# Two feed-forward column groups from seven products of summed blocks instead of eight

## Chip, cores and metric

The kernel runs on one core of a Trainium2 chip. The metric is device time in microseconds (us), the median of several runs of the same program. A core has TensorE (PE in the profile; PEld is its weight load), VectorE (DVE), ScalarE (ACT), GpSimd (POOL) and SyncE (SP, which here issues nearly all DMAs). PE reads operands from SBUF and writes to eight banks of PSUM; a bank holds 128 x 512 float32 numbers.

## What is computed

A trunk of two layers over 256 tokens of width 1024. Each layer is a half-step SwiGLU feed-forward (FFN), a token mixer, and a second FFN, each followed by a layer norm:

```
def swiglu(x, w_gate, w_up, w_down):
    return (jax.nn.silu(x @ w_gate) * (x @ w_up)) @ w_down

for l in range(2):
    x = layer_norm(ALPHA * x + 0.5 * swiglu(x, ffn1_gate[l], ffn1_up[l], ffn1_down[l]), ...)
    mix = ...      # pooling heads and a gated recurrence, then @ w_out[l]
    x = layer_norm(ALPHA * x + mix, ...)
    x = layer_norm(ALPHA * x + 0.5 * swiglu(x, ffn2_gate[l], ffn2_up[l], ffn2_down[l]), ...)
```

The hidden width of an FFN is 2816. All is float32.

## The kernel before

**Numbers in two halves.** PE multiplies in a rounded 32-bit format (`fp32r`). To keep float32 accuracy each operand is split into a high part (a cast on ACT) and a low part (the remainder, a subtraction on DVE); the helper `halves` (lines 115-117) does both. A product is then three matmuls, high x high, high x low and low x high, issued by `mm3` (lines 109-113) for a 128 x 128 by 128 x 512 block.

**Groups.** An FFN works through eleven groups (`NG`) of 256 hidden columns. A group's gate and up columns lie side by side, so 1024 input rows x 512 columns, which is four tiles of 128 x 1024 float32 (512 KB each, two input blocks of 128 rows per tile). The 256 tokens are two row blocks (`hf` 0 and 1). Two forms make a group's gate and up products:

- `G(g, hf)`: tokens of one row block are the stationary operand, the 512 columns move. The result is token-major, so SiLU x up (`hn`) is turned by two PE transposes (`T`, lines 455-463) before the down product can use it.
- `GT(g)`: weights are stationary and the tokens move, both row blocks and both halves at once: 32 matmuls of 512 columns (weights' high part against the tokens' high and low parts) and 32 of 256 columns (weights' low part). The result is already hidden-major and needs no transpose. `gate_turned` (lines 358-370) evacuates it.

`D(g, hf)` is the group's share of the down product for one row block: 12 matmuls of 512 columns, accumulated in PSUM over all groups (pool `psa`).

**Order.** PE runs in the written order (`manual_schedule`). The later three FFNs (all but the first one of layer 0) run `G` for groups 0, 1 and 10 and `GT` for groups 2 to 9; from group 3 on each `GT(g)` is followed by both halves of `D(g-1)`. `Later` is a small queue that counts steps (one tick for each three 512-column matmuls) and puts transposes between them, so many ticks behind what they need. ACT, DVE and SP are ordered by the compiler's list scheduler from priorities: evacuations ahead (`AHEAD`), weight loads behind (`BEHIND`).

**Loads.** `Weight.load` issues one DMA into a buffer of the `raw` pool (five buffers), then the ACT cast and the DVE subtraction into a pair of buffers of a ring: `w` (eight), `x` (two more, within an FFN) for gate and up, `d` (six) for down weights. A ring buffer comes free when PE has done its last matmul on it; a `raw` buffer when both parts have been made. The loads stand in one list for the whole program.

**Banks.** Pool `psg` has four PSUM banks: one for each `G`, four for each `GT`, one for each transpose step.

Of the kernel before, what the change touches and what calls it, by code (L numbers as in the profile page):

```python
# [17 lines left out]
P = 128  # L18
# [15 lines left out]
PAD = 16  # L34
TINY = 2.0 ** -60
NEG = -1e30
RAW, NW, NX, ND = 5, 8, 2, 6
FFN_BELOW = ("xh", "xl", "sil", "hn", "zero")
MIX_BELOW = ("mth", "mtl", "la", "lb", "pw", "v", "P01", "Pm")
AHEAD, BEHIND = 100, 400  # L40
PINNED, STARTED = 4, 4
HT = 6
MAPPED = 13
WARM = 17

# [31 lines left out]
def trunk(ctx: ExitStack, tc: tile.TileContext, t, out: bass.AP):  # L77
# [28 lines left out]
            for g in self.guards:  # L106
                g.__exit__(None, None, None)

    def mm3(ps, lh, ll, wh, wl, start, stop):
        nc.tensor.matmul(ps, lh, wh, start=start, stop=False)  # L110
        nc.tensor.matmul(ps, lh, wl, start=False, stop=False)  # L111
        nc.tensor.matmul(ps, ll, wh, start=False, stop=stop)  # L112
        later.tick()

    def halves(dst_h, dst_l, src):
# [5 lines left out]
    class Weight:  # L121


        def __init__(self, src, ring, bufs, by_hand=False):
            self.src, self.ring, self.bufs, self.by_hand = src, ring, bufs, by_hand
            self.uses = 2
            self.parts = None
            stream.append(self)

        def load(self):  # L130
            p = wp if self.ring == "w" else scope[0]
            older = rings.setdefault(self.ring, []) if p else None
# [44 lines left out]
    place = [0, 1]  # L177

    class Transposed:
        def __init__(self, hf, nat, slots=(), cuts=(0, 4, 8)):  # L180
            self.h, self.l = xth[:, place[hf]], xtl[:, place[hf]]
            self.nat, self.cuts, self.done = nat, list(cuts), 0
            for n in slots:

                later(n - 1, lambda: later(1, self.part))

        def part(self):
            a, b = self.cuts[0], self.cuts[1]
            pt = psg.tile([P, 4 * P], F32, name="gu").rearrange("p (k t) -> p k t", k=4)
            for k in range(a, b):  # L190
                nc.tensor.transpose(pt[:, k - a, :], self.nat[:, k * P:(k + 1) * P], ident)  # L191
            halves(self.h[:, a:b, :], self.l[:, a:b, :], pt[:, 0:b - a, :])
            self.done = b
            self.cuts.pop(0)

    def project(hf, ps, ws):

# [51 lines left out]

    normed = [None]  # L250

    def layer_norm(hf, accs, scale, gb, slots, last=False):
        z = xp.tile([P, D], F32, name="x")
        st = sp.tile([P, 2, 6], F32, name="st")
        mv = sp.tile([P, 2], F32, name="mv")
        rs = sp.tile([P, 1], F32, name="rs")
        for c in range(2):
            cs = slice(c * 512, c * 512 + 512)
            nc.vector.scalar_tensor_tensor(z[:, cs], accs[c], scale, x[hf][:, cs], ALU.mult, ALU.add)
            nc.vector.bn_stats(st[:, c, :], z[:, cs])  # L260
        nc.vector.bn_aggr(mv, st.rearrange("p a b -> p (a b)"))
        nc.vector.tensor_scalar_add(rs, mv[:, 1:2], LN_EPS / ALPHA ** 2)
        nc.gpsimd.tensor_tensor(rs, rs, neghalf[:, 0:1], ALU.pow)
        for c in range(2):
            cs = slice(c * 512, c * 512 + 512)
            nc.vector.scalar_tensor_tensor(z[:, cs], z[:, cs], mv[:, 0:1], gb[0][:, cs], ALU.subtract, ALU.mult)
            normed[0] = nc.vector.scalar_tensor_tensor(z[:, cs], z[:, cs], rs, gb[1][:, cs], ALU.mult, ALU.add)
            if last:
                nc.sync.dma_start(out[hf * P:(hf + 1) * P, cs], z[:, cs])
        x[hf] = z  # L270
        pinned[0] = PINNED
        if not last:
            xT[hf] = Transposed(hf, z, slots)

    def last_norm(hf, scale, gb, parts, half, right):

# [25 lines left out]
    class FFN:  # L302
        def __init__(self, l, w, ln_i, first=False, last=False):
            gu, dn = t["gu"][l, w], t["dn"][l, w]
            self.first, self.last, self.mixer_next = first, last, not w
            self.slots = ((16, 16), (14, 14) if w else (13, 13))
            self.accs = [None, None]
            self.gw, self.dw, self.ht = {}, {}, {}
            self.ln = (l, ln_i)
            self.gb = None  # L310
            for g in range(NG):
                self.gw[g] = []
                for kq in range(4):
                    extra = (4 * g + kq) % (NW + NX) >= NW
                    self.gw[g].append(Weight(gu[g, kq], *(("x", NX) if extra else ("w", NW)), first and g == 0))
                for n in {0: [], 1: [0, 1], 2: [], NG - 1: [NG - 2, NG - 1]}.get(g, [g - 1]):
                    self.dw[n] = [Weight(dn[2 * n + i], "d", ND) for i in range(2)]

        def G(self, g, hf):
            ps = psg.tile([P, 2 * GW], F32, name="gu")  # L320
# [3 lines left out]
        def GT(self, g):  # L324

            later.wait(lambda: self.turned(g - 1) or all((g - 1, hf) in self.ht for hf in range(2)))
            ps = [[psg.tile([P, 2 * S], F32, name="gu") for _ in range(2)] for _ in range(2)]
            n = 0  # L330
            for lo in range(2):
                w = S if lo else 2 * S

                blocks = [[0], [1]] if lo or g == 2 and not self.first else [[0, 1]]
                for block in blocks:
                    for kt in range(KT):
                        later.wait(lambda: min(xT[0].done, xT[1].done) > kt)
# [14 lines left out]
                    if lo:  # L352
                        self.gate_turned(g, block[0], ps[block[0]])

        def turned(self, g):
            return (0 if self.first else 2) <= g < NG - 1

        def gate_turned(self, g, i, ps):
            gate = scope[0].tile([P, S], F32, name="sil", bufs=2)
# [12 lines left out]
        def gate(self, g, hf, ps):  # L372
# [82 lines left out]
        def T(self, g, hf, hn):  # L455
# [5 lines left out]
            with tc.high_priority(offset=AHEAD):  # L461
                halves(hth, htl, pt)
            self.ht[g, hf] = (hth, htl)

        def D(self, g, hf, cols=(0, 1)):
            if self.turned(g):
# [15 lines left out]
            for c in cols:  # L482
                cs = slice(c * 512, c * 512 + 512)
                for i in range(2):
                    mm3(self.accs[hf][c], ht[i][0], ht[i][1], dw[i][0][:, cs], dw[i][1][:, cs],
                        g == 0 and i == 0, i == 1 and g == NG - 1 - (self.last and hf == 1 and c == 1))
            if 1 not in cols:
                return
            for w in self.dw[g]:
                w.used()  # L490
            if g == NG - 1:
                layer_norm(hf, self.accs[hf], 0.5 / ALPHA, self.gb, self.slots[hf], self.last)

        def run(self):
            G, GT, D = self.G, self.GT, self.D
            if self.first:
                self.start()
                D(0, 0)
                D(0, 1)
                GT(2)  # L500
                D(1, 0)
                D(1, 1)
            else:
                G(0, 0)
                G(1, 0)
                D(0, 0)
                G(0, 1)
                G(1, 1)
                D(1, 0)
                D(0, 1)  # L510
                GT(2)
                D(1, 1)
            for g in range(3, NG - 1):
                GT(g)
                D(g - 1, 0)
                if g < NG - 2:
                    D(g - 1, 1)
            G(NG - 1, 0)
            D(NG - 2, 0)
            D(NG - 1, 0)  # L520
            G(NG - 1, 1)
            if self.mixer_next:
                tc.keep_in_program_order(nc.scalar.preload_act_table_set("natural_log_exp_and_others"))
            if self.first:
                with tc.high_priority(offset=-BEHIND):
                    lower_bounds()
            if self.last:

                for g, cols in ((NG - 3, (0,)), (NG - 2, (0,)), (NG - 3, (1,)), (NG - 1, (0,)), (NG - 2, (1,)), (NG - 1, None)):
                    D(g, 1, cols)  # L530
            else:
                for g in range(NG - 3, NG):
                    D(g, 1)

        def end(self, ht, dw):

# [58 lines left out]
    def mixer(l, win, wout):  # L595
# [295 lines left out]
        for hf in range(2):  # L891
# [12 lines left out]
                wout[kt].used()  # L904
            if hf == 0:
                place.reverse()
            layer_norm(hf, accs, 1.0 / ALPHA, gb, (14, 14) if hf else (13, 13))

    phases = []
    for l in range(DEPTH):  # L910
# [88 lines left out]
```

## Time and profile before

| | |
|---|---|
| median of 3 runs | 949.76 us (949.13 to 950.33) |
| the profiled execution | 949.23 us |
| its span, first to last instruction | 947.5 us |
| PE busy | 937.8 us, 4911 matmuls |
| DVE busy | 653.4 us |
| ACT busy | 515.1 us |
| DMA | 180.05 MB, mean 190 GB/s |
| granted PE clock | 0.998 |

The profile follows one execution. A matmul's duration there is the time from its start to the end of its last result; successive matmuls overlap, so what a matmul costs is read from the distance between starts.

### The profile page before, as it was taken

The page shows a single profiled execution, that of the slowest core. Times are in us where ns is not written, and L with a number is a line of the kernel's source. Part 1 is how long each engine was busy: PE and PEld are TensorE (multiplying, and loading weights), DVE is VectorE, ACT ScalarE, POOL GpSimd, SP SyncE. Part 2 cuts the span into 40 slices and gives each one's busy share as a digit, 9 for nine tenths or more (in the row PEclk, how much of TensorE's full clock was granted, in tenths as well). Part 3 has the DMA queues.
Part 4 walks back from the last instruction along what each step waited for, and adds up shares of the span by engine and source line. Part 5 has one row for each costly group of instructions (what it writes and reads, how often), then busy time and mean ns, then how long its engine had stood idle before and what let it go on. Part 6 is the DMA issues. An engine that isn't in the chain of part 4 may idle for free.

```text
span 947.5 us, 13287 instructions
## 1 busy us (share of the span) xinstructions
PE 937.8 (99%) x4911; PEld 803.9 (85%) x4911; DVE 653.4 (69%) x1089; ACT 515.1 (54%) x816; POOL 22.7 (2%) x38
## 2 busy tenths in 40 slices
PE   9999999999999999999999999999999999999996
PEld 7888888888988888888888888888898888888885
DVE  7885666779879765655776565647899797565625
ACT  7765554368546755454546645533975466646420
POOL 0000000000010000000000000000000000000000
PEclk9999999999999999999999999999999999999999
DMA  8987676333627876655446666542417377666301
GB/s 307 319 273 262 239 238 196 105 108 115 228 88 254 300 242 208 211 183 178 139 150 244 221 226 211 166 153 101 150 51 264 118 267 263 221 229 213 114 1 45
DMA packets 50944, 180.05 MB, mean 190 GB/s; under 512 B 6208, under 2 KB 6464, under 8 KB 50880
## 3 DMA queue, kind: packets, MB, share of 16 engines
q1 hardware_dynamic: 50544, 178.55, 55.9%
q8 instruction: 38, 0.62, 0.3%
q0 software_dynamic: 192, 0.53, 0.2%
q14 instruction: 26, 0.21, 0.1%
q10 hardware_dynamic: 144, 0.13, 0.0%
HBM read 178.14 MB, written 1.05 MB: 189 GB/s over the span
## 4 chain that ended last, share of the span: by engine, by line
PE 97%; DVE 1%; DMA 1%; ACT 0%; issue 0%; DVEq 0%; ACTq 0%
PE gu L343 39%; PE acc L112 10%; PE acc L111 10%; PE acc L110 10%; PE gu L110 7%; PE gu L111 7%; PE gu L112 7%; PE gu L837 1%; PE acc L418 1%; PE gu L191 1%; PE acc L763 1%; PE acc L709 1%; DMA raw<-in_wout 1%; PE gu L458 0%; PE gu L442 0%; PE acc L799 0%
## 5 line engine op out<-in xcount | busy, mean ns | idle before, releaser
L116 ACT CAST wh<-raw 128x1024 fp32r<-128x1024 f32 x196 | 205.3, 1053 | 112.0 <-DMA raw<-in_gu 41.7
L117 DVE TENSOR_TENSOR wl<-raw,wh 128x1024 fp32r<-128x1024 f32 x196 | 236.1, 1219 | 21.9 <-ACT wh L116 13.9
L343 PE MATMUL gu<-xt,wh 128*128 128x512 f32 x800 | 187.8, 390 | 0.0
L343 PEld LDWEIGHTS gu<-xt,wh 128*128 128x128 f32 x800 | 150.1, 188 | 31.9
L117 DVE TENSOR_TENSOR dl<-raw,dh 128x1024 fp32r<-128x1024 f32 x88 | 106.7, 1222 | 99.4 <-ACT dh L116 99.4
L116 ACT CAST dh<-raw 128x1024 fp32r<-128x1024 f32 x88 | 92.2, 1052 | 115.3 <-DMA raw<-in_dn 105.5
L110 PE MATMUL acc<-dh,hth 128*128 128x512 f32 x354 | 138.6, 392 | 0.0
L112 PE MATMUL acc<-dh,htl 128*128 128x512 f32 x354 | 137.9, 390 | 0.0
L111 PE MATMUL acc<-dl,hth 128*128 128x512 f32 x354 | 137.6, 389 | 0.0
L110 PE MATMUL gu<-wh,xt 128*128 128x512 f32 x288 | 114.1, 396 | 0.0
L111 PE MATMUL gu<-wl,xt 128*128 128x512 f32 x288 | 112.4, 390 | 0.0
L112 PE MATMUL gu<-wh,xt 128*128 128x512 f32 x288 | 112.4, 390 | 0.0
L343 PE MATMUL gu<-xt,wl 128*128 128x256 f32 x800 | 103.8, 283 | 0.0
L343 PEld LDWEIGHTS gu<-xt,wl 128*128 128x128 f32 x800 | 101.0, 192 | 1.9
L366 DVE TENSOR_TENSOR sil<-gu,sil 128x256 f32<-128x256 f32 x66 | 27.7, 420 | 86.9 <-ACT sil L365 86.7
L112 PEld LDWEIGHTS acc<-dh,htl 128*128 128x128 f32 x354 | 66.5, 188 | 13.8
L110 PEld LDWEIGHTS acc<-dh,hth 128*128 128x128 f32 x354 | 66.6, 188 | 12.1
L111 PEld LDWEIGHTS acc<-dl,hth 128*128 128x128 f32 x354 | 66.5, 188 | 12.2
L112 PEld LDWEIGHTS gu<-wh,xt 128*128 128x128 f32 x288 | 54.1, 188 | 11.7 <-DVE xt L117 0.2
L111 PEld LDWEIGHTS gu<-wl,xt 128*128 128x128 f32 x288 | 54.2, 188 | 10.7
L110 PEld LDWEIGHTS gu<-wh,xt 128*128 128x128 f32 x288 | 54.1, 188 | 10.6
L343 PE MATMUL gu<-xt,xh 128*128 128x512 f32 x256 | 61.3, 390 | 0.0
(187 smaller groups left out, 1071.1 us busy)
## 6 DMA issues: line engine op xcount, KB each, us to landing
raw<-in_gu SPq DMA_DIRECT2D x172, 512.0 KB, 4.4
raw<-in_dn SPq DMA_DIRECT2D x88, 512.0 KB, 4.5
raw<-in_win SPq DMA_DIRECT2D x40, 512.0 KB, 4.1
raw<-in_wout SPq DMA_DIRECT2D x16, 512.0 KB, 5.0
lng<-in_ln_g SPq DMA_DIRECT2D x6, 512.0 KB, 5.4
lnb<-in_ln_b SPq DMA_DIRECT2D x6, 512.0 KB, 6.4
x<-in_first SPq DMA_DIRECT2D x4, 384.0 KB, 3.9
raw<-in_first SPq DMA_DIRECT2D x4, 384.0 KB, 5.5
```

What stands on the lines that cost most here:

```text
L110: nc.tensor.matmul(ps, lh, wh, start=start, stop=False)
L111: nc.tensor.matmul(ps, lh, wl, start=False, stop=False)
L112: nc.tensor.matmul(ps, ll, wh, start=False, stop=stop)
L116: first = nc.scalar.copy(dst_h, src)
L117: return first, nc.vector.tensor_tensor(dst_l, src, dst_h.bitcast(F32), ALU.subtract)
L191: nc.tensor.transpose(pt[:, k - a, :], self.nat[:, k * P:(k + 1) * P], ident)
L343: nc.tensor.matmul(ps[i][part][:, 2 * S - w:], weight.parts[lo][:, c:c + P], x[:, 0:w], start=kt == 0 and not lo, stop=kt == KT - 1 and lo ...
L366: nc.vector.tensor_tensor(dst, p[:, 0:S], dst, ALU.add)
L418: nc.tensor.matmul(ps[i][part][:, 2 * S - w:], ws[k // 2].parts[lo][:, c:c + P], xs[:, 0:w], start=k == 0 and not lo, stop=k == KT - 1 and ...
L709: nc.tensor.matmul(pe[:, a:], lf[hf][c][:, h * P:(h + 1) * P], cumM[:, c, a:], start=True, stop=True)
L763: nc.tensor.matmul(dst[:, 2 * j:2 * j + 2, :], side[:, j, :], E[:, 2 * j:2 * j + 2, t0:t0 + dst.shape[2]], start=True, stop=True)
L837: nc.tensor.matmul(ps[i // 2][:, i % 2, :], w, x, start=kt == 0 and n == 0 and i % 2 == 0, stop=kt == KT - 1 and n == 2 and i % 2 == 1)
```

## The change

In each of the three later FFNs the gate and up products of groups 6 and 7 are made together. Take the 256 tokens as two row blocks, the two groups as two column blocks of 512, and the 1024 input rows as two blocks (the even and the odd blocks of 128). The product of two 2 x 2 block matrices takes eight block products; here it takes seven (the scheme of Strassen and Winograd), some of them of sums and differences of blocks. Of these, three are made in the steps `A6.0` to `A6.3` (9 matmuls each step) and four in `B6.0` to `B6.3` (12 each). Their results are token-major: four `T` steps turn them, at 5, 8, 10 and 11 ticks after the last `B` step.

- The sums of token blocks are made on DVE behind each layer norm that leads into a later FFN (`full_part`), from an ACT copy of the transposed tokens, and are split into `Sh` and `Sl`.
- The sums of weight blocks are made on DVE in the `raw` buffers, ahead of cast and subtraction (`first_sums`, `later_sums`). Steps `A` use six loads and steps `B` eight, where the two groups took eight.
- The order of the later FFNs is written out. The down products of groups 2, 3, 4 and 5 are kept back and stand between and behind the `A` and `B` steps. `D0.0` moves from ahead of `G0.1` to behind `G1.1`.
- Loads are listed in the order in which PE's steps need them, in all four FFNs (`share`). The `x` ring stays in the first FFN alone, with three buffers; the later FFNs have the eight of `w`. `hth` and `htl` have eight buffers each, not six.

The core of the diff:

```diff
-RAW, NW, NX, ND = 5, 8, 2, 6
+RAW, NW, NX, ND = 5, 8, 3, 6
+ORDER = [... for s in (
+    "G0.0 G1.0 G0.1 G1.1 D0.0 D0.1 T2 D1.0 T3 D1.1 T4 D2.0 T5 D2.1 "
+    "A6.0 A6.1 A6.2 A6.3 D3.0 B6.0 D3.1 B6.1 D4.0 B6.2 B6.3 D4.1 D5.0 D5.1 T8 D6.0 D6.1 T9 D7.0 D7.1 D8.0 G10.0 D9.0 D10.0 G10.1 ").split()]
+TURNS = (5,8,10,11)
-HT = 6
+HT = 8
...
+                if self.mix:
+                    self.mix(raw)
                 first, second = halves(wh, wl, raw)
...
             halves(self.h[:, a:b, :], self.l[:, a:b, :], pt[:, 0:b - a, :])
+            if self.full:
+                self.full(a // 4, pt)
...
+    def full_part(n, part, pt):
+        own = scope[0].tile([P, 4, P], F32, name="cb", bufs=4)
+        nc.scalar.copy(own, pt)
+        parts_seen[n, part] = own
...
+        if (1 - n, part) in parts_seen:
+            (a11, a12), (a21, a22) = ([parts_seen[i, part][:, k::2] for k in range(2)] for i in range(2))
+            raw = rawp.tile([P, 4, 2, P], F32, name="raw")
+            for dst, a, b, op in ((0, a21, a22, ALU.add), (2, a11, a21, ALU.subtract), (1, raw[:, 0], a11, ALU.subtract),
+                                  (3, a12, raw[:, 1], ALU.subtract)):
+                nc.vector.tensor_tensor(raw[:, dst], a, b, op)
+            sh, sl = (s[:, :, 2 * part:2 * part + 2] for s in sums[0])
+            halves(sh, sl, raw)
...
+    def first_sums(raw, left):
+        for i in range(2):
+            cs = slice(i * 512, i * 512 + 512)
+            nc.vector.tensor_tensor(raw[:, cs], raw[:, cs], left[i].raw[:, 0:512], ALU.subtract)
+
+    def later_sums(raw, right):
+        if right is None:
+            nc.vector.tensor_tensor(raw[:, 0:512], raw[:, 512:], raw[:, 0:512], ALU.subtract)
+        else:
+            nc.vector.tensor_tensor(raw[:, 0:512], right.raw[:, 0:512], raw[:, 0:512], ALU.add)
+            nc.vector.tensor_tensor(raw[:, 512:], raw[:, 0:512], raw[:, 512:], ALU.subtract)
...
+        def A(self, g, n):
+            if n == 0:
+                later.wait(lambda: not self.pending)
+                self.banks = [psg.tile([P, 512], F32, name="gu") for _ in range(3)]
...
+            mm3(self.banks[0], xth[:, 0, k], xtl[:, 0, k], wh[:, 0:512], wl[:, 0:512], start, stop, True)
+            mm3(self.banks[1], xth[:, 0, k + 1], xtl[:, 0, k + 1], wh[:, 512:], wl[:, 512:], start, stop, True)
...
+            mm3(self.banks[2], *self.sums(0, n), th, tl, start, stop, True)
...
+            with tc.high_priority(offset=AHEAD):
+                c11, self.p5 = (scope[0].tile([P, 512], F32, name="cb", bufs=4) for _ in range(2))
+                nc.scalar.copy(c11, self.banks[0])
+                nc.vector.tensor_tensor(c11, c11, self.banks[1], ALU.add)
+                nc.scalar.copy(self.p5, self.banks[2])
...
+        def B(self, g, n):
+            if n == 0:
+                self.banks[1:2] = [psg.tile([P, 512], F32, name="gu") for _ in range(2)]
+            x, z, w, y = self.banks
...
+            products = [lambda: mm3(z, *self.sums(2, n), *t3, start, stop, True),
+                        lambda: mm3(y, *self.sums(3, n), *b22, False, stop, True),
+                        lambda: mm3(x, *self.sums(1, n), *t2, False, stop, True)]
+            for m in (2, 0, 1) if stop else (0, 1, 2):
+                products[m]()
...
+            mm3(w, xth[:, 1, 2 * n + 1], xtl[:, 1, 2 * n + 1], *t4, start, stop, True)
...
+            with tc.high_priority(offset=AHEAD):
+                u, v = (scope[0].tile([P, 512], F32, name="cb", bufs=4) for _ in range(2))
+                nc.scalar.copy(u, x)
+                nc.vector.tensor_tensor(v, u, z, ALU.add)
+                nc.vector.tensor_tensor(u, u, y, ALU.add)
+                nc.vector.tensor_tensor(self.p5, self.p5, v, ALU.add)
+                nc.vector.tensor_tensor(v, v, w, ALU.subtract)
...
+        def by_block(self, g):
+            return not self.first and g in (2,8)
```

In the step names a number ahead of the point is the group (6 stands for the pair 6 and 7), the one behind it the row block or, for `A` and `B`, the step; `T2` in this list is `GT(2)`. `by_block` makes `GT(2)` and now `GT(8)` finish one half of the group's high-part matmuls before the other, so that only two banks are needed at first.

More of the change, by code (lines that the diff above doesn't have):

```diff
@@ L107, in close, with mm3 @@
                 g.__exit__(None, None, None)
[L109 to L112, printed above, removed]
+    def mm3(ps, lh, ll, wh, wl, start, stop, more=False):
+        for n, (a, b) in enumerate(((lh, wh), (lh, wl), (ll, wh))):
+            nc.tensor.matmul(ps, a, b, start=start and n == 0, stop=stop and n == 2, skip_group_check=more)
         later.tick()
@@ L272, in layer_norm @@
         if not last:
-            xT[hf] = Transposed(hf, z, slots)
+            xT[hf] = Transposed(hf, z, slots, full=full and (lambda part, pt, n=place[hf]: full(n, part, pt)))
     def last_norm(hf, scale, gb, parts, half, right):
@@ L310, in __init__ @@
             self.gb = None
[L311 to L317, printed above, removed]
+            self.plan = list(self.order())
@@ new lines, in __init__, with share, want @@
+            self.pairs = {step[1] for step in self.plan if step[0] == "A"}
+            self.pending = set()
+            self.share(gu, dn)
+        def share(self, gu, dn):
+            cost = {"G": 24, "GT": 48, "D": 12, "A": 9, "B": 12}
+            wanted, when, start = [], 0, {}
+            def want(src, begin, end, kind=None, mix=None):
+                wanted.append([src, begin, end, kind, mix])
+                return len(wanted) - 1
+            ends = {}
+            for what, g, *rest in self.plan:
+                n = cost[what] // (2 if rest[1:] and rest[1] and len(rest[1]) == 1 else 1)
+                ends[what, g] = when + n
+                when += n
+            when, sets = 0, {}
+            for what, g, *rest in self.plan:
+                n = cost[what]
+                if what == "B":
+                    sets[what, g, rest[0]] = [want(gu[g + 1, rest[0]], when, when + n, None, "right"),
+                                              want(gu[g, rest[0]], when, when + n, None, "left")]
+                elif what == "A":
+                    if not rest[0] % 2:
+                        k = rest[0]
+                        sets[what, g, k] = [want(gu[g, k], when, when + n, None, "keep"),
+                                            want(gu[g, k + 1], when, when + 2 * n, None, "keep"),
+                                            want(gu[g + 1, k:k + 2, :, 0:512].rearrange("k p c -> p k c"),
+                                                 when, when + 2 * n, None, "first")]
+                elif (what, g) not in sets:
+                    begin, end = when, ends[what, g]
+                    if what in ("G", "GT"):
+                        sets[what, g] = [want(gu[g, k], begin, end) for k in range(4)]
+                    elif what == "D":
+                        sets[what, g] = [want(dn[2 * g + i], begin, end, "d") for i in range(2)]
+                when += cost[what] // (2 if rest[1:] and rest[1] and len(rest[1]) == 1 else 1)
+            free = {"w": [-12] * NW, "x": [-12] * (NX if self.first else 0), "d": [-8] * ND}
+            size = {"w": NW, "x": NX, "d": ND}
+            made = []
+            for n, (src, begin, end, kind, mix) in enumerate(wanted):
+                ring = "d" if kind == "d" else "w" if n < 4 or not self.first else min("wx", key=lambda r: free[r][0])
+                free[ring] = free[ring][1:] + [end]
+                how = None
+                if mix == "first":
+                    how = lambda raw, left=made[-2:]: first_sums(raw, left)
+                elif mix == "right":
+                    how = lambda raw: later_sums(raw, None)
+                elif mix == "left":
+                    how = lambda raw, right=made[-1]: later_sums(raw, right)
+                made.append(Weight(src, ring, size[ring], self.first and n < 4, how))
+            for (what, *where), of in sets.items():
+                ws = [made[n] for n in of]
+                if what in ("G", "GT"):
+                    self.gw[where[0]] = ws
+                elif what == "D":
+                    self.dw[where[0]] = ws
+                else:
+                    self.gw[(what, *where)] = ws
@@ new lines, in order @@
+        def order(self):
+            if self.first:
+                yield "G", 0, 0
+                yield "GT", 1
+                yield from (("D", 0, 0), ("D", 0, 1), ("GT", 2), ("D", 1, 0), ("D", 1, 1))
+                for g in range(3, NG - 1):
+                    yield "GT", g
+                    yield "D", g - 1, 0
+                    if g < NG - 2:
+                        yield "D", g - 1, 1
+            else:
+                yield from ORDER
+                if self.last:
+                    yield from (("D", g, 1, cols) for g, cols in ((FINAL[0], (0,)), (FINAL[1], (0,)), (FINAL[0], (1,)),
+                                                                  (NG - 1, (0,)), (FINAL[1], (1,)), (NG - 1, None)))
+                else:
+                    yield from (("D", g, 1) for g in (*FINAL, NG - 1))
+                return
+            yield "G", NG - 1, 0
+            yield "D", NG - 2, 0
+            yield "D", NG - 1, 0
+            yield "G", NG - 1, 1
+            yield from (("D", g, 1) for g in range(NG - 3, NG))
@@ L324, in GT @@
         def GT(self, g):
-            later.wait(lambda: self.turned(g - 1) or all((g - 1, hf) in self.ht for hf in range(2)))
+            later.wait(lambda: not self.pending)
             ps = [[psg.tile([P, 2 * S], F32, name="gu") for _ in range(2)] for _ in range(2)]
@@ L332, in GT @@
                 w = S if lo else 2 * S
-                blocks = [[0], [1]] if lo or g == 2 and not self.first else [[0, 1]]
+                blocks = [[0], [1]] if lo or self.by_block(g) else [[0, 1]]
                 for block in blocks:
@@ L491, in D @@
             if g == NG - 1:
-                layer_norm(hf, self.accs[hf], 0.5 / ALPHA, self.gb, self.slots[hf], self.last)
+                layer_norm(hf, self.accs[hf], 0.5 / ALPHA, self.gb, self.slots[hf], self.last,
+                           None if self.mixer_next else full_part)
         def run(self):
[L495 to L533, printed above, removed]
+            for what, *args in self.plan:
+                if what == "G" and self.first and args[0] == 0:
+                    self.start()
+                elif what == "GT" and self.first and args[0] == 1:
+                    pass
+                else:
+                    getattr(self, what)(*args)
+                if args[:2] == [NG - 1, 1] and what == "G":
+                    if self.mixer_next:
+                        tc.keep_in_program_order(nc.scalar.preload_act_table_set("natural_log_exp_and_others"))
+                    if self.first:
+                        with tc.high_priority(offset=-BEHIND):
+                            lower_bounds()
         def end(self, ht, dw):
```

72 lines of the change are left out of this document (61 added, 11 removed).

## The prediction

> **What bounds the kernel now.** I read the page first: busy times, then the chain that ended last.
>
> ```profile
> span 947.5 us, 13287 instructions
> ...
> PE 937.8 (99%) x4911; PEld 803.9 (85%) x4911; DVE 653.4 (69%) x1089; ACT 515.1 (54%) x816; POOL 22.7 (2%) x38
> ...
> PE 97%; DVE 1%; DMA 1%; ACT 0%; issue 0%; DVEq 0%; ACTq 0%
> ```
>
> PE is the whole chain. Whether it ever waits is read from windows (columns: stretch, length, then busy us of PE, PEld, DVE, ACT and POOL, granted clock, DMA share, GB/s):
>
> ```profile
> 60.00:930.00 870.00, 869.15 (x4549) 745.38 (x4548) 597.87 (x1004) 470.73 (x747) 21.00 (x30) 1.00 0.55 184
> 365.60:382.20 16.60, 16.60 (x90) 14.37 (x89) 9.78 (x15) 8.88 (x14) 0.00 (x0) 1.00 0.72 254
> 329.70:332.50 2.80, 2.80 (x15) 2.31 (x14) 2.80 (x7) 1.95 (x6) 0.00 (x0) 1.00 0.82 278
> 281.00:305.00 24.00, 24.00 (x117) 20.00 (x116) 23.37 (x31) 15.32 (x20) 1.00 (x1) 1.00 0.76 241
> 318.60:343.60 25.00, 25.00 (x142) 21.94 (x141) 16.28 (x22) 16.90 (x26) 0.00 (x0) 1.00 0.74 250
> 0.00:60.00 60.00, 58.94 (x317) 50.44 (x318) 47.53 (x68) 43.59 (x69) 0.74 (x7) 1.00 0.90 312
> ```
>
> PE is idle 0.85 us of 870, at full clock. So only PE work taken out can shorten the kernel, and any wait put in lengthens it. One GT with its two D (16.6 us) leaves DVE 6.8 us free, but around a layer norm (281 to 305) DVE is busy 23.37 of 24.
>
> **PE's price list.** The chain in order of time gives a GT; the timeline of PE gives the rest (start, duration of what is merged in the row).
>
> ```profile
> 365.77 11.11 PE gu L343 x64
> ```
> ```profile
> 274.83 0.39 PE L110 MATMUL acc<-wh,xt 128*128 128x512 f32 x1
> ...
> 283.44 0.39 PE L112 MATMUL acc<-wh,xt 128*128 128x512 f32 x1
> ...
> 296.37 1.04 PE L191 MATMUL gu<-ident,x 128*128 128x128 f32 x8
> ...
> 298.64 0.39 PE L110 MATMUL acc<-dh,hth 128*128 128x512 f32 x1
> ...
> 302.53 0.39 PE L112 MATMUL gu<-wh,xt 128*128 128x512 f32 x1
> 302.76 0.38 PE L458 MATMUL gu<-ident,hn 128*128 128x128 f32 x2
> 302.89 0.48 PE L110 MATMUL gu<-wh,xt 128*128 128x512 f32 x1
> 303.21 0.39 PE L111 MATMUL gu<-wl,xt 128*128 128x512 f32 x1
> ```
>
> - A 512-column matmul: from 274.83 to 283.44 are 38 steps between 39 matmuls, 0.2266 us each (its duration, 0.39, overlaps the next).
> - A T step (two transposes): from the last matmul before it (302.53) to the second behind it (303.21) 0.68 us, where two plain steps take 0.45: 0.23 us.
> - One GT: 11.11 us. One D, 12 matmuls: 2.72 us.
>
> **The sum on PE.** Removed per later FFN: GT(6) and GT(7), 22.22 us. Added: 4 x 9 in A and 4 x 12 in B, 84 matmuls, 19.03 us, and four T, 0.92 us. The D, G, layer norm transposes and the other GT are moved, not changed. Gain 22.22 - 19.03 - 0.92 = 2.27 us, times three FFNs 6.8 us. The profiled execution, 949.23 us, becomes 942.4; the median, 949.76, is 0.53 higher than that execution and becomes 943.0 if PE never waits.
>
> [...] The row of the transposes:
>
> ```profile
> L458 PE MATMUL gu<-ident,hn 128*128 128x128 f32 x40 | 7.7, 272 | 0.0
> ```
>
> Their mean duration is 272 ns. [...]
>
> **What must now be hidden: DVE and loads in the A and B stretch.** The rows of a cast and of DVE's operations (busy us, mean ns of one, idle before), then timeline rows, some of them merged pairs:
>
> ```profile
> L116 ACT CAST wh<-raw 128x1024 fp32r<-128x1024 f32 x196 | 205.3, 1053 | 112.0 <-DMA raw<-in_gu 41.7 <-PE gu L112 27.3 <-PE gu L343 13.6
> L117 DVE TENSOR_TENSOR wl<-raw,wh 128x1024 fp32r<-128x1024 f32 x196 | 236.1, 1219 | 21.9 <-ACT wh L116 13.9 <-PE gu L343 7.1
> L117 DVE TENSOR_TENSOR xt<-gu,xt 128x512 fp32r<-128x512 f32 x20 | 12.9, 683 | 3.4 <-ACT xt L116 3.4
> L366 DVE TENSOR_TENSOR hn<-gu,hn 128x256 f32<-128x256 f32 x66 | 27.3, 414 | 0.0
> ```
> ```profile
> 285.59 1.28 DVE L117 TENSOR_TENSOR xt<-gu,xt 128x512 fp32r<-128x512 f32 x2
> ...
> 299.01 1.28 DVE L117 TENSOR_TENSOR xt<-gu,xt 128x512 fp32r<-128x512 f32 x2
> ...
> 375.34 0.42 DVE L366 TENSOR_TENSOR sil<-gu,sil 128x256 f32<-128x256 f32 x1 [3.31 <-ACT sil L365]
> 375.68 0.41 DVE L366 TENSOR_TENSOR hn<-gu,hn 128x256 f32<-128x256 f32 x1
> ...
> 380.28 2.35 DVE L117 TENSOR_TENSOR wl<-raw,wh 128x1024 fp32r<-128x1024 f32 x2
> ```
>
> Back to back, a weight remainder takes 2.35 - 1.22 = 1.13 us, a 512-wide operation 1.28 - 0.68 = 0.60, a 256-wide one 0.34.
>
> The step with least room is B6.3. Four of the six A loads fit in the ring while GT(5) runs on the other four buffers; the rest start as GT(5) frees them. Its last 16 matmuls are of 256 columns, (11.11 - 32 x 0.2266) / 32 = 0.12 us each, and the first buffer is free after four of them, 1.4 us ahead of its end. From its end to B6.3, PE runs D2.1, A (36), D3.0, B6.0 to B6.2 (36), D3.1 and D4.0: 120 matmuls, 27.2 us; with the 1.4, 28.6 us. Due by then on DVE: two A loads, eight B loads and four down weights, 14 x 1.13 = 15.8 us; the block sums, 2 for R23 (the second `first_sums` load) and 4 x 3 for B, 14 x 0.60 = 8.4; what is left of GT(5)'s evacuation and A's own, 4 x 0.34 + 0.60 + 0.34 = 2.3. Together 26.5 us in 28.6: 93% busy, more than any GT stretch of before, less than the 97% at 281 to 305. At worst each operation costs its mean duration: 14 x 1.219 + 14 x 0.683 + 5 x 0.414 + 0.683 = 29.4 us; at 97% that is 30.3, and B6.3 waits 1.7 us. At best the sums run early, in raw buffers that need no free ring buffer, and it waits nothing. I take 0.5 us for each FFN, nearer the best, since back-to-back rows show what a full DVE does: 1.5 us. The cover is DVE's 6.8 free us in each GT before; if it is gone, PE pays one for one.
>
> [...] The rows show starts 0.08 us ahead of the end before.
>
> Behind B: c11, u, p5 and v need five 512-wide operations (one already counted) and four SiLU products, some 4 us on DVE at high priority. The T steps come 5 to 11 ticks (3.4 to 7.5 us) behind, while D4.1, D5.0 and D5.1 run 8.2 us: nothing. Queued weight work can delay each by at most one 1.22.
>
> ACT gains eight casts and some ten copies over an FFN; it was busy 8.88 of 16.6 us, so nothing. Were that cover gone, a cast would cost 1.05 us.
>
> **Loads.** Six more per FFN, 9.4 MB in all, and `D4.0` now sits inside B, so the two layer norm vectors (two more 512 KB on SP's queue) fall near that stretch.
>
> ```profile
> raw<-in_gu SPq DMA_DIRECT2D x172, 512.0 KB, 4.4
> ...
> lnb<-in_ln_b SPq DMA_DIRECT2D x6, 512.0 KB, 6.4
> ```
>
> The first 60 us moved 312 GB/s, a load each 1.68 us. Sixteen loads by B6.3 take 27 us at that rate, of which up to five wait landed in `raw`: hidden. SP's in-order waits for a raw buffer hold back later loads only. POOL's queue is untouched.
>
> **The start of an FFN.** `full_part` adds 8 x 0.34 + 2 x 1.13 = 5 us of DVE there; the next stretch (318 to 343) has 8.7 free. But D0.0 stood between the second row block's transposes and G0.1 as cover. In the rows above they start at 296.37, D0.0 at 298.64, and the first low part is made by DVE at 299.01 + 0.68 = 299.69. G0.1's third matmul needs it at 298.64 + 0.45 = 299.09: a wait of 0.6 us, in the two FFNs behind a mixer. If the sums (4 x 0.34 + 1.13 = 2.5 us) also come ahead of the second low part, made at 300.29 and needed 2.7 us later than the first: 302.8 against 301.8, 1.0 us. Between 0 (DVE puts it first) and 1.0 I take 0.5, twice: 1.0 us.
>
> **Other moves at nothing.** GT now follows GT with one D between three times per FFN, and A follows GT(5) so; before it was once; the row 329.70:332.50 shows PE full over such a gap, with DVE also full. If a remainder cuts in, 1.13 us each. The smaller ring: with eight buffers a GT's loads start when the GT before the last frees its four, a GT and a D (13.8 us) ahead, and need 4.4 us to land, one cast and 4 x 1.13, some 10 us. Only the list order of the first FFN's loads changes; PE was full there with DMA at 90% of its time (0 to 60), so I cost it at nothing too, where a late load would cost up to the 1.68 us between loads.
>
> Sum: -6.8 + 1.5 + 1.0 = -4.3, the profiled execution 944.9, the median 945.5 us.
>
> **Rivals.**
> - *DVE leaves gaps in the A and B stretch, and it gets slower.* The order on DVE is fixed beforehand and each remainder waits for its cast:
>
> ```profile
> DVE dl L117 <- ACT dh L116: 99.4, 57, 6.4
> ```
>
>   99.4 us of DVE idling of this kind exist already, 1.7 us a time. At 80% busy, 26.5 us take 33.1 and B6.3 waits 4.5 us per FFN: 949.8 - 6.8 + 13.5 + 1.0 = 957.5. It turns slower where the three waits exceed 6.8 + 1.9 - 1.0 = 7.7 us, 2.6 each, that is DVE under 85%. For: the GT row has DVE at 59%. Against: there it has less to do. Chance 0.16.
> - *DVE pays full durations*: waits of 1.7: 949.8 - 6.8 + 5.1 + 1.0 = 949.1, no change. Against: the 2.35 row. 0.07.
> - *Raw buffers bound the loads.* A load of B that waits for its partner holds its buffer for at most 6.4 us to land, 1.7 for the partner, 1.2 for sums, 1.05 and 1.13 for cast and remainder, 11.5 us; were all 14 held so, five buffers would take 32.2 us and be 3.6 late, and at the 4.4 us of a plain load (9.5 us held) 26.6, in time. Half of that, 1.8 late: 949.8 - 6.8 + 5.4 + 1.0 = 949.4, no change. For: sums hold two or three buffers together. Against: down weights have no sums. 0.08.
> - *Transposes cost their duration*: 8 x 0.272 = 2.18 us, gain 1.01 per FFN, 949.8 - 3.0 + 2.5 = 949.3, no change. 0.03.
>
> **How the numbers follow.** 0.2% (1.9 us) is about what a measurement can tell from no change. The forecast has 0.66: 943.0 (no waits) to 947.4, its own range. No change: 0.07 + 0.08 + 0.03 = 0.18. Slower 0.16. The range takes in the no-change cases and ends at 951.5, where the slower one begins, which it leaves out; below it starts at 942.5, half a us under the waitless sum.
>
> **What would show it.** In the profile after: 84 matmuls in 19.0 us of starts for A and B; T steps still at 0.23; DVE over 90% from GT(5) to B6.3; PE idle, if any, in front of B6.3 or G0.1. Wrong it is if PE stops elsewhere, in front of a T or a GT, or if waits exceed 2.6 us per FFN.

## The result and the profile after

The changed kernel takes 945.02 us (median of six), the kernel before 949.29 us on the same chip. One of the six executions ran at a lower granted clock (0.849, 1029 us); without it the median is 944.78 us, and the ratio of the others to the kernel before is 0.9948, 95% interval 0.9934 to 0.9961. The forecast was 945.5. The profiled execution takes 944.78 us, its span is 942.8.

The page after (span; busy times; the chain that ended last):

```profile
span 942.8 us, 13184 instructions
...
PE 932.9 (99%) x4803; PEld 794.6 (84%) x4803; DVE 719.2 (76%) x1176; ACT 540.4 (57%) x837; POOL 23.1 (2%) x38
...
PE 88%; DVE 4%; DMA 4%; issue 1%; ACT 1%; SPq 0%; DVEq 0%; ACTq 0%
```

PE has 108 matmuls fewer and is busy 4.9 us less; DVE has 66 us more to do. The chain shows what that used up: before, it ran through PE for 97% of the span, now for 88%, and the rest is weights on their way through DMA, ACT and DVE.

Windows of the kernel after (columns as in the prediction): the long stretch, and the A and B stretch of the second FFN, from the start of D2.1 to just ahead of the first T step:

```profile
60.00:930.00 870.00, 869.57 (x4470) 740.61 (x4469) 663.71 (x1092) 496.89 (x770) 21.46 (x30) 1.00 0.58 196
369.60:402.00 32.40, 32.40 (x144) 26.65 (x143) 31.07 (x41) 19.61 (x26) 0.00 (x0) 1.00 0.77 248
```

PE stands for 0.43 us of 870, and in the A and B stretch for none, with DVE busy 31.07 of 32.40 us (96%).

PE's timeline after: the layer norm transposes that open and close the second FFN, the ends of the A and B stretch, and the two places where PE waited in a later FFN:

```profile
297.62 1.04 PE L200 MATMUL gu<-ident,x 128*128 128x128 f32 x8
...
369.62 0.39 PE L117 MATMUL acc<-dh,hth 128*128 128x512 f32 x1
...
402.99 0.39 PE L117 MATMUL acc<-dh,htl 128*128 128x512 f32 x1
403.22 0.38 PE L658 MATMUL gu<-ident,cb 128*128 128x128 f32 x2
403.36 0.48 PE L117 MATMUL acc<-dh,hth 128*128 128x512 f32 x1
403.67 0.39 PE L117 MATMUL acc<-dl,hth 128*128 128x512 f32 x1
...
467.18 1.04 PE L200 MATMUL gu<-ident,x 128*128 128x128 f32 x8
...
592.14 0.40 PE L540 MATMUL gu<-xt,wh 128*128 128x512 f32 x1
592.78 1.43 PE L540 MATMUL gu<-xt,wh 128*128 128x512 f32 x5 [0.24 <-DVE htl L122]
...
764.42 0.39 PE L117 MATMUL gu<-wl,xt 128*128 128x512 f32 x1
764.74 0.74 PE L117 MATMUL gu<-wh,xt 128*128 128x512 f32 x2
```

- From 369.62 to 403.22 lie 147 steps (D2.1, A and B with D3.0, D3.1 and D4.0 between them, D4.1 and the first three matmuls of D5.0): 33.60 us, 0.2286 each, against 0.2266 for plain ones. Nothing stands there.
- A T step: 402.99 to 403.67 is 0.68, two plain steps are 0.45: 0.23 us, as before.
- From transposes to transposes the second FFN takes 467.18 - 297.62 = 169.56 us. Before, its rows start at 296.37 (shown in the prediction) and 468.11: 171.74. It is 2.18 us shorter.

```profile
468.11 1.03 PE L191 MATMUL gu<-ident,x 128*128 128x128 f32 x8
```

- The second bank of GT(8) comes 0.64 us after the first matmul (592.14 to 592.78) instead of 0.23: it waits for `htl` of the last T step, whose bank it takes.

From such rows the difference of the two executions, 5.1 us up to the last matmul, splits into:

| | us |
|---|---|
| first FFN (slower first matmuls, 1.89 us for four in place of 1.35; one wait in a GT) | +1.29 |
| first mixer | -0.04 |
| second FFN | -2.18 |
| third FFN (0.52 at GT(8), 0.18 in A) | -1.31 |
| second mixer, which had stood 1.1 us before | -1.07 |
| fourth FFN (0.2 at G0.1) | -1.81 |

Behind the last matmul the changed kernel takes 0.48 us longer to its end (8.49 us, before 8.01), so of the 5.1 us the span keeps 4.7. The rows up to the issue of the output's DMA are alike; the 0.48 us lie between that issue and the end, and why is not settled.

### The profile page after: what moved, and what is told of

Read it like the earlier page. It is cut to its first block, busy times and chain, and to the rows that moved or that the text cites. A ratio compares the mean times of both kernels' runs of the same rounds, so it can differ in the third digit from the quotient of the medians.

```text
span 942.8 us, 13184 instructions
## 1 busy us (share of the span) xinstructions
PE 932.9 (99%) x4803; PEld 794.6 (84%) x4803; DVE 719.2 (76%) x1176; ACT 540.4 (57%) x837; POOL 23.1 (2%) x38
## 4 chain that ended last, share of the span: by engine, by line
PE 88%; DVE 4%; DMA 4%; issue 1%; ACT 1%; SPq 0%; DVEq 0%; ACTq 0%
PE gu L540 28%; PE acc L117 26%; PE gu L117 25%; PE gu L1013 2%; DMA raw<-in_dn 2%; DMA raw<-in_cumM 1%; PE acc L618 1%; DVE wl L122 1%; PE acc L939 1%; DMA raw<-in_gu 1%; PE gu L200 1%; PE acc L885 1%; DVE dl L122 1%; PE gu L658 1%; PE acc L975 0%
## 5 line engine op out<-in xcount | busy, mean ns | idle before, releaser
L121 ACT CAST wh<-raw 128x1024 fp32r<-128x1024 f32 x237 | 248.1, 1053 | 155.6 <-DMA raw<-in_gu 53.2
L122 DVE TENSOR_TENSOR wl<-raw,wh 128x1024 fp32r<-128x1024 f32 x237 | 286.0, 1221 | 36.9 <-ACT wh L121 18.9
L117 PE MATMUL gu<-wh,xt 128*128 128x512 f32 x648 | 213.3, 394 | 0.0
L117 PEld LDWEIGHTS gu<-wh,xt 128*128 128x128 f32 x648 | 121.6, 188 | 25.4 <-DVE xt L122 0.5
L117 PE MATMUL gu<-wl,xt 128*128 128x512 f32 x324 | 126.5, 391 | 0.0
L117 PEld LDWEIGHTS gu<-wl,xt 128*128 128x128 f32 x324 | 61.0, 188 | 12.1
L566 DVE TENSOR_TENSOR sil<-gu,sil 128x256 f32<-128x256 f32 x54 | 22.7, 420 | 61.6 <-ACT sil L565 61.6
L121 ACT CAST hth<-hn 128x256 fp32r<-128x256 f32 x56 | 22.7, 406 | 18.6 <-DVE hn L568 17.9
L576 ACT ACTIVATE sil<-gu 128x256 f32<-128x256 f32 x20 | 7.7, 383 | 43.8 <-PE gu L117 43.6
L565 ACT COPY sil<-gu 128x256 f32<-128x256 f32 x54 | 19.9, 369 | 16.8 <-PE gu L540 16.7
```

The lines of the kernel that those rows point to most:

```text
L117: nc.tensor.matmul(ps, a, b, start=start and n == 0, stop=stop and n == 2, skip_group_check=more)
L121: first = nc.scalar.copy(dst_h, src)
L122: return first, nc.vector.tensor_tensor(dst_l, src, dst_h.bitcast(F32), ALU.subtract)
L565: nc.scalar.copy(dst, p[:, S:2 * S])
L566: nc.vector.tensor_tensor(dst, p[:, 0:S], dst, ALU.add)
```

## Experiments

Ratios are to the kernel before, on the same chip, with a 95% interval. Changes are against the changed kernel.

**The same kernel again**, twice: its ratio beside the other runs.

> The changed kernel itself, once more, as the base for the other runs and as a second look at where its time goes. If the 6.8 us of PE work are the gain and the rest of the ledger (a slower start, one wait of 0.5 us in the first FFN, one of 0.5 us at GT(8) of the second later FFN) belongs to this execution and not to the kernel, those waits come elsewhere or not at all, and the later FFNs again lose 1.8 to 2.2 us each. If the waits belong to the change, they stand in the same places: 0.5 us at 116.7 and at 592.1 us.

> The changed kernel once more, unchanged, as the measure for the two runs beside it on the same chip. Every theory: a ratio to the kernel before of 0.995, about 944 to 945 us.

944.06 us, 0.9951 (0.9939 to 0.9964), and 944.04 us, 0.9939 (0.9927 to 0.9951). A wait at GT(8) came back in both (0.43 and 0.26 us in the third FFN); the one in the first FFN did not, and that FFN was 0.72 and 0.63 us longer than before, not 1.29. The second FFN was 1.57 and 2.12 us shorter, the first with 0.57 us of waits in its GT steps. The 0.48 us behind the last matmul are there in both.

**Groups 6 and 7 as GT again**, without sums of tokens or weights; the rest is kept: written order, load list, ring, buffers.

```diff
-    "A6.0 A6.1 A6.2 A6.3 D3.0 B6.0 D3.1 B6.1 D4.0 B6.2 B6.3 D4.1 D5.0 D5.1 T8 ..."
+    "T6 D3.0 D3.1 T7 D4.0 D4.1 D5.0 D5.1 T8 ..."
```

> Keeps the new order, load list, rings and eight hidden-part buffers, but makes groups 6 and 7 by two GT again, each followed by its down products, and no block sums. Theory (the gain is the matmuls that the seven products spare): PE's work is that of before, so 949.3 us within 1 us. Rival (the new order and load list are worth something themselves): faster than before by over 1 us, about 947, or slower by the lost cover at G0.1, about 950.5.

950.13 us, 1.0014 (1.0001 to 1.0028). The new order and list gain nothing (by the interval they cost 0.1 to 2.7 us). The seven products are the whole gain: 950.13 - 944.06 = 6.1 us.

**Down products not kept back**: D(g-1) behind GT(g) as before, none between A and B, only D5 behind B.

```diff
-    "... T2 D1.0 T3 D1.1 T4 D2.0 T5 D2.1 A6.0 ... A6.3 D3.0 B6.0 D3.1 B6.1 D4.0 B6.2 B6.3 D4.1 D5.0 D5.1 T8 ..."
+    "... T2 D1.0 D1.1 T3 D2.0 D2.1 T4 D3.0 D3.1 T5 D4.0 D4.1 A6.0 ... A6.3 B6.0 B6.1 B6.2 B6.3 D5.0 D5.1 T8 ..."
```

> Keeps the seven products but does not keep the down products back: D follows its GT as before, A and B stand side by side, D5.0 and D5.1 alone come behind. Theory (DVE's work due by B6.3 is hidden only since D2.1, D3 and D4 stand in between): from the end of GT(5) PE passes D4, A and B6.0 to B6.2 in 21.8 us and, with the 1.4 us before it, has 23.2; DVE owes 2 + 8 loads and D5's two, 12 x 1.13 + 14 x 0.60 + 2.3 = 24.3 us, 25.0 at 97%: a wait of some 1.8 us in or ahead of B, and the last two T come before GT(8) with no down product over them, some 0.7 us: 2.5 us per FFN, 7.5 in all, about 952.5. Rival (the order hides nothing that matters): 945 as the changed kernel.

958.01 us, 1.0097 (1.0083 to 1.0112): slower than before, and 5.5 us over what was expected. Its timeline behind B in the second FFN, and windows there:

```profile
406.75 0.39 PE L117 MATMUL acc<-dh,htl 128*128 128x512 f32 x1
407.66 0.77 PE L658 MATMUL gu<-ident,cb 128*128 128x128 f32 x4 [0.52 <-DVE cb L510]
410.53 0.69 PE L658 MATMUL gu<-ident,cb 128*128 128x128 f32 x2 [2.10 <-DVE cb L510]
410.87 1.63 PE L540 MATMUL gu<-xt,wh 128*128 128x512 f32 x3
```
```profile
399.10:406.90 7.80, 7.80 (x37) 6.28 (x35) 6.59 (x8) 4.89 (x6) 0.00 (x0) 1.00 0.92 345
406.90:411.00 4.10, 1.48 (x9) 0.88 (x7) 4.05 (x9) 3.98 (x9) 0.00 (x0) 0.91 0.77 253
411.00:414.50 3.50, 3.50 (x12) 2.79 (x11) 3.50 (x5) 1.93 (x4) 0.00 (x0) 0.61 0.76 206
```

PE does not stop in front of B (no step of A or B is over 0.3 us late) but in front of the T steps, for `cb`: DVE is full (4.05 of 4.10 us) and eight ticks of down products are too few for the products of c11, u, p5 and v. Then comes a cost that no term had: the granted clock falls (0.61 is the mean of the last window), and matmuls start 0.43 us apart instead of 0.23 for some 3 us.

**No down products between A and B, but D4 and D5 behind B**: D3 comes ahead of A.

```diff
-    "... T2 D1.0 T3 D1.1 T4 D2.0 T5 D2.1 A6.0 ... A6.3 D3.0 B6.0 D3.1 B6.1 D4.0 B6.2 B6.3 D4.1 D5.0 D5.1 T8 ..."
+    "... T2 D1.0 D1.1 T3 D2.0 T4 D2.1 T5 D3.0 D3.1 A6.0 ... A6.3 B6.0 B6.1 B6.2 B6.3 D4.0 D4.1 D5.0 D5.1 T8 ..."
```

> As the run with A and B side by side, but D4 comes behind B instead of ahead of A, so that D4.0, D4.1, D5.0 and D5.1 stand behind it (16 ticks for four T steps), and none between A and B. Theory (what the kept-back down products are needed for is the evacuation behind B: copy, four additions and three SiLU products on a full DVE, some 3 us longer than I had it): the waits at T vanish, B waits at most 0.3 us, and the time is the changed kernel's, 944 to 945. Rival (down products between A and B are needed too, for ACT's copies of two banks and for DVE's sums): 1 to 2 us of waits in front of B6.0 or B6.3 per FFN and a slower clock behind them, 948 to 953.

949.57 us, 0.9999 (0.999 to 1.0009): in the range of the rival. The trace is of the longest of twelve executions (947.17 to 951.69 us). Its timeline at B6.3 of the second FFN, and windows ahead of it and behind:

```profile
394.22 0.39 PE L117 MATMUL gu<-wh,xt 128*128 128x512 f32 x1
394.89 0.50 PE L117 MATMUL gu<-wh,Sh 128*128 128x512 f32 x1 [0.28 <-ACT wh L121]
397.12 0.50 PE L117 MATMUL gu<-wl,Sh 128*128 128x512 f32 x1 [1.73 <-DVE wl L122]
```
```profile
371.00:394.50 23.50, 23.50 (x107) 18.77 (x105) 21.76 (x30) 13.86 (x21) 0.00 (x0) 1.00 0.61 200
394.50:403.00 8.50, 6.49 (x21) 4.83 (x21) 7.31 (x9) 5.01 (x6) 0.00 (x0) 0.80 0.94 308
```

This is the wait at B6.3 that the prediction named, 0.44 + 2.01 us, with matmuls 0.43 us apart behind it (1.6 us more; the granted clock is 0.80 in the second window); in the third and fourth FFN PE waits there for 1.5 and 0.8 us. But the run before has no down products between A and B either, and does not wait at B6.3. What differs is how many halves of down products PE has passed by then, and how many are left behind B:

| | ahead of B6.3 | behind B, ahead of GT(8) | where PE waits in the second FFN |
|---|---|---|---|
| not kept back | 10 | 2 | T steps, 0.7 + 2.3 us |
| the changed kernel | 9 | 3 | nowhere |
| D4 and D5 behind B | 8 | 4 | B6.3, 0.44 + 2.01 us |

Ahead of B6.3 the down products stretch the time in which DVE prepares weights; behind B they stretch the time in which it makes the outputs. Both are needed; that those ahead must stand between A and B is not shown.

**Each sum of weight blocks followed by another operation of its size** on the same `raw` part, four such lines:

```diff
             nc.vector.tensor_tensor(raw[:, cs], raw[:, cs], left[i].raw[:, 0:512], ALU.subtract)
+            nc.vector.tensor_tensor(raw[:, cs], raw[:, cs], raw[:, cs], ALU.max)
```

> Behind each block sum of the weights stands one more DVE operation of the same size in place (the maximum of a number with itself): 14 x 0.60 = 8.4 us more DVE work due by B6.3, 16 x 0.60 = 9.6 per FFN. Theory (DVE is 93 to 97% full there, so added work goes one for one into PE's waits once the small room is used): 34.9 us at 97% are 36.0 against 28.6, up to 7.4 us per FFN less what runs early while GT(5) goes on (some 2 us): 5.4 per FFN, 16 in all, about 961. Rival (DVE has room since its sums run far ahead in raw buffers): under 3 us in all, about 947.

970.54 us, 1.0228 (1.0213 to 1.0244), 9.5 us over what was expected. PE's timeline at B6.2 and B6.3, DVE's row at the end of the long wait, and a window behind:

```profile
394.93 0.39 PE L117 MATMUL gu<-wh,Sh 128*128 128x512 f32 x1
396.16 0.50 PE L117 MATMUL gu<-wl,Sh 128*128 128x512 f32 x1 [0.85 <-DVE wl L122]
...
397.20 0.40 PE L117 MATMUL gu<-wh,xt 128*128 128x512 f32 x1
401.49 0.79 PE L117 MATMUL gu<-wh,Sh 128*128 128x512 f32 x1 [3.89 <-ACT wh L121]
402.74 0.79 PE L117 MATMUL gu<-wl,Sh 128*128 128x512 f32 x1 [0.47 <-DVE wl L122]
```
```profile
401.46 1.23 DVE L122 TENSOR_TENSOR wl<-raw,wh 128x1024 fp32r<-128x1024 f32 x1 [1.16 <-ACT wh L121]
```
```profile
401.40:407.50 6.10, 5.55 (x13) 4.03 (x14) 6.04 (x6) 5.36 (x7) 0.00 (x0) 0.52 0.68 230
```

This measures the room. Fourteen more operations of 0.60 us are due by B6.3, 8.4 us. PE stands for 1.01 + 0.11 + 4.06 + 1.03 + 0.37 = 6.6 us of them at B6.2 and B6.3 (excess of the steps over 0.2266), so about 1.8 us had been free; the same count gives 0.8 and 1.6 us in the third and fourth FFN. It is a rough measure: the last two steps are already at about half clock (0.52 in the window from 401.40 on), some 0.4 us of the count, and at the end DVE itself stands 1.16 us for a cast of ACT, which lies between a sum and its remainder. The prediction's account (26.5 us due in 28.6) left 2.1. The rest of the loss, some 1.8 us in the second and fourth FFN, is again the lower clock (0.52 in that window of the second FFN).

**Without those sums**, the same four lines left out, one shown:

```diff
-            nc.vector.tensor_tensor(raw[:, cs], raw[:, cs], left[i].raw[:, 0:512], ALU.subtract)
+            pass
```

> Leaves out the sums of weight blocks (16 DVE operations of 512 columns per later FFN), so A and B multiply plain blocks; PE, ACT and DMA do all they did. The run with doubled sums put 6.4 us of waits on each FFN for 8.4 us of added work due by B6.3, so some 2.0 us of room were left there. Theory (at the changed kernel's load DVE is full but PE does not wait for it): 944.1 us as the changed kernel, within 1 us. Rival (DVE's sums already cost PE the difference between 6.8 us and the measured gain): about 942, 2 us faster than the changed kernel.

944.14 us, 0.9942 (0.993 to 0.9954), the same as with them. In this order the sums of weights cost nothing that can be measured.

**Two pairs per FFN**, groups 4 and 5 and groups 7 and 8; groups 6 and 9 become `G`, and only `GT(2)` still finishes one half first:

```diff
+    "G0.0 G1.0 G0.1 G1.1 D0.0 T2 D0.1 T3 D1.0 A4.0 A4.1 A4.2 A4.3 D1.1 B4.0 D2.0 B4.1 D2.1 B4.2 B4.3 D3.0 D3.1 "
+    "G6.0 G6.1 D4.0 D4.1 A7.0 A7.1 A7.2 A7.3 D5.0 B7.0 D5.1 B7.1 D6.0 B7.2 B7.3 D6.1 G9.0 G9.1 D7.0 ..."
```

> Two pairs in each later FFN, 4 and 5 and 7 and 8, each with one down product or more between its steps; groups 6 and 9 in the token-major form behind B, where their matmuls cover the evacuation. PE: one more pair spares 2.27 us, two GT turned into G cost 2 x (10.88 + 0.46 - 11.11) = 0.46: 1.8 us less per FFN, 5.4 in all. Theory (DVE has free time outside the stretch, 785 us of 940 with two pairs, and the order spreads it): 944.1 - 5.4 = 938.7, within 1.5 us. Rival (DVE is the bound once two stretches follow each other): waits over 1 us at a B step, each followed by some 1.5 us of slow clock, 945 or more.

949.78 us, 1.0008 (1.0 to 1.0017): 11 us over the expectation. PE's waits (who waited for what, us in total, times, longest), a window over its second FFN, and one over that of the changed kernel:

```profile
PE gu L658 <- DVE cb L510: 3.8, 8, 1.3
PE gu L117 <- DVE htl L122: 1.4, 2, 1.2
...
PE acc L618 <- ACT wh L633: 0.5, 1, 0.5
PE gu L658 <- DVE hn L577: 0.4, 1, 0.4
PE gu L540 <- DVE sil L566: 0.3, 1, 0.3
```
```profile
297.00:470.00 173.00, 170.26 (x788) 138.34 (x787) 146.23 (x192) 101.74 (x141) 0.92 (x1) 1.00 0.71 244
```
```profile
297.00:467.00 170.00, 170.00 (x853) 144.01 (x852) 132.78 (x183) 101.37 (x148) 0.92 (x1) 1.00 0.68 230
```

By the prices of the prediction its 4623 matmuls would take 5.4 us less than those of the changed kernel, as expected. The time is in the range of the rival, but no B step waits and the clock stays full (1.00 in the window). Its T steps, as many ticks behind B as in the changed kernel, wait instead, for `cb`: DVE is busy 146 of 173 us (85%) in place of 133 of 170 (78%), and comes later with the outputs.

**Two pairs, groups 3 and 4 and groups 6 and 7**, with groups 5 and 8 as `G`:

```diff
+    "G0.0 G1.0 G0.1 G1.1 D0.0 T2 D0.1 A3.0 A3.1 A3.2 A3.3 D1.0 B3.0 D1.1 B3.1 D2.0 B3.2 B3.3 D2.1 G5.0 G5.1 D3.0 D3.1 "
+    "D4.0 A6.0 A6.1 A6.2 A6.3 D4.1 B6.0 D5.0 B6.1 D5.1 B6.2 B6.3 G8.0 G8.1 D6.0 D6.1 T9 D7.0 ..."
```

> Two pairs, 3 and 4 and 6 and 7, with groups 5 and 8 token-major behind B; the first pair starts behind GT(2), nearer to the layer norm. Theory: the same PE work as with pairs 4 and 7, 938.7. Rival (DVE, full around the layer norm and now with the token sums there too, is late for the first pair): waits in A3 or B3 of 1 to 3 us with slow clock behind, 943 to 950, slower than pairs 4 and 7.

954.1 us, 1.0048 (1.0035 to 1.0061), slower than the theory and than the rival's 943 to 950. Its longest waits:

```profile
PE gu L117 <- ACT cb L495: 6.5, 3, 2.9
```

Line 495 is the copy of `u` behind B: G8.0, which comes straight behind B6.3, waits for a bank. Nothing stands behind B as cover. The rival had put the waits into A or B.

**Two pairs (4, 5 and 7, 8) with later T steps**:

```diff
-TURNS = (5,8,10,11)
+TURNS = (8,12,15,18)
```

> Two pairs, groups 4 and 5 and groups 7 and 8, as in the two-pair run, only with the T steps behind a B issued 8, 12, 15 and 18 ticks after it instead of 5, 8, 10 and 11, so that most of them stand inside the G steps that follow. In the trace of the two-pair run TensorE stood for 2.6, 1.5 and 2.1 us per FFN (6.2 us together) in front of those T steps, for sums of products that VectorE had not finished. Theory (the two-pair run lost its gain to these T steps coming too early for VectorE): those waits go, 949.8 - 6.2 = 943.6 us, about the level of the changed kernel. Rival (VectorE, 80% busy, is behind altogether, and a wait taken away at one place comes back at the next): 947 to 950 us, with the waits at B, A or GT steps instead.

**The same, and each D of the first half one place later**, only D3.1 behind B:

```diff
-    "... D0.0 T2 D0.1 T3 D1.0 A4.0 ... A4.3 D1.1 B4.0 D2.0 B4.1 D2.1 B4.2 B4.3 D3.0 D3.1 G6.0 ..."
+    "... D0.0 D0.1 T2 D1.0 T3 D1.1 A4.0 ... A4.3 D2.0 B4.0 D2.1 B4.1 D3.0 B4.2 B4.3 D3.1 G6.0 ..."
```

> As the run with the later T steps, and in the first half of the FFN each down product moved one place later: both of D0 ahead of GT(2), so that there are 5.4 us instead of 2.7 between G1.1 and GT(2), and only D3.1 behind B. Theory (every wait is one late step with too little cover of its own): the wait of 0.57 us at GT(2) in the second FFN and the 0.5 us at GT(3) shrink too, up to 1 us below the run with the later T steps, 942.6 to 943.6. Rival (VectorE is behind altogether): no gain over that run, or a loss, since the stretch of B itself is not relieved.

948.1 us, 0.9984 (0.9974 to 0.9994), and 958.0 us, 1.0076 (1.0059 to 1.0093). The first lies in the range of the rival (VectorE behind altogether): the T steps no longer wait for `cb`, but of the 6.2 us only 1.7 were gained (2.3 by the ratios, since the chips differ), because the next consumer now stands. The second lost 10 us more. Waits of the first, then of the second:

```profile
PE acc L117 <- DVE htl L122: 1.8, 2, 0.9
...
PE gu L658 <- DVE htl L122: 1.0, 2, 0.6
PE gu L117 <- ACT cb L466: 0.8, 2, 0.6
PE gu L658 <- DVE hn L577: 0.7, 2, 0.3
PE acc L117 <- ACT hth L121: 0.4, 1, 0.4
```
```profile
PE acc L117 <- ACT hth L121: 6.6, 4, 2.3
```

A T step issued later is later for the down product that reads it (`hth`, `htl`). In the second kernel two ticks lie between the last T step of groups 4 and 5 and D4.0, where the first had six, and PE stands there for 1.75 and 0.66 us. At D7.0 both have two ticks; there the waits of the second and third FFN grew from 1.65 and 1.09 to 2.4 and 2.5 us, and why is not settled. One pair is the best version that was found.

## Why the prediction was right, and where only the sum was

- **PE's sum**: held. Predicted 2.27 us per FFN; the second FFN, which had no wait to speak of, became 2.18 shorter. A and B ran at 0.2286 a step (0.2 us over the 84 matmuls more than priced), a T step took 0.23 us. A single transpose of `cb` lasts 0.271 us (median of 24); its duration as its price would have left a gain of about 1.0 us per FFN by the prediction's estimate, and the 2.18 us decide against it. The rival of transposes at their full duration fell.
- **The wait at B6.3** (1.5 us in the sum): not there. The account of DVE (2.1 us free in 28.6) agrees with the doubled sums as far as they can tell: 1.8 us in the second FFN, 0.8 and 1.6 in the others. So the place was the right one to fear, and the wait came when eight halves of down products stood ahead of B6.3 in place of nine. The term of 0.5 per FFN was mis-sized: with room left it is 0. The rivals with full DVE durations and with `raw` buffers, which put waits of 1.7 and 1.8 us there, fell with it.
- **The start of an FFN** (1.0 us): 0.2 us, in the fourth FFN alone.
- **The term of nothing behind B** failed. GT(8) takes the bank of the last T step; where DVE makes `htl` late, its second bank is late: 0.52 us in the third FFN here, 0.35, 0.43 and 0.05 us in the three FFNs of the next execution. A stop of PE in front of a GT is what the prediction said would prove it wrong; its size was a fifth of the 2.6 us per FFN that would have turned the gain. With one half of a down product fewer there (D4.1), in the run without kept-back products, PE stood 0.7 + 2.3 us in front of the T steps.
- **The total**: waits in the later FFNs came to 1.5 us (2.3 and 1.6 in the two repeats), not 2.5, and the gain there to 5.3 us (4.5 and 5.2), not 4.3. That the forecast came within 0.5 us is partly luck: it owes something to terms that the sum did not have, the first FFN's +1.29, the second mixer's -1.07 and the 0.48 us behind the last matmul.
- **The slower rival** (DVE leaves gaps): fell for this order, DVE is busy 96% of the stretch. With D4 and D5 behind B, B6.3 waits although DVE is at 93% (21.76 of 23.50 us): there the cover is too short, and not DVE under the 85% that this rival needed.
- **The price of a wait** was taken as the wait itself. Behind 2.0 to 4.1 us of standing it was, in four of the runs, 1.4 to 2.3 us more, as told below, so the 957.5 us of the slower rival, with 4.5 us per FFN, was probably too low.

## What to carry to other kernels

When the bounding engine loses work, do the account of the next engine between the loads' first free buffer and the step that needs them: here it left 2.1 us of 28.6, and adding work measured some 1 to 2. Kept-back work of the bounding engine has to be shared between two places, ahead of the step that needs operands and behind the step that leaves results. A second saving of the same kind is not worth its sum if it uses up the same kept-back work. A step moved later to give its producer time takes that time from its own consumer.

## What was not expected of the hardware

A wait of PE can cost more than its length. Behind 2.0 to 4.1 us of standing, matmuls started 0.43 us apart instead of 0.23 for 3.4 us, or 6.8 us with the sums doubled, at a granted clock of 0.50, which adds 1.4 to 2.3 us. This came in all three later FFNs with the sums doubled (mean granted clock of the execution 0.988, where the changed kernel has 0.998), in all three without kept-back products (0.992), in the second FFN with D4 and D5 behind B (0.995), where 0.44 + 2.01 us sufficed, and twice in the slowest kernel with two pairs (0.995; 0.73 in the window from 437.80 to 444.20 around one of them). Two stretches of the run without kept-back products, in which PE stands for 2.38 and 2.41 us, with the ones behind them (columns as in the prediction, granted clock third from the end):

```profile
406.88:410.29 3.41, 1.03 (x6) 0.40 (x4) 3.36 (x7) 3.29 (x8) 0.00 (x0) 1.00 0.87 281
410.29:413.70 3.41, 3.17 (x9) 2.59 (x10) 3.41 (x7) 2.46 (x4) 0.00 (x0) 0.50 0.70 190
594.61:598.02 3.41, 1.00 (x6) 0.40 (x4) 3.13 (x7) 3.41 (x9) 0.00 (x0) 1.00 0.83 286
598.02:601.43 3.41, 3.17 (x9) 2.59 (x10) 3.41 (x7) 2.74 (x5) 0.00 (x0) 0.50 0.66 197
```

But length alone does not decide: with groups 3, 4, 6 and 7 paired, PE stood 3.1 us and went on at a granted clock of 1.00.

```profile
593.50:600.00 6.50, 3.55 (x16) 2.65 (x15) 4.93 (x6) 4.41 (x5) 0.00 (x0) 1.00 1.00 371
```

Why one wait was followed by the lower clock and the other not is not settled.
